# A depthwise convolution's VectorE taps read from a copy in PSUM, with tap counts, weight lows and norm operands moved

## The chip, the cores and the metric

The kernel runs on one core of a Trainium2 chip. The metric is device microseconds (us) of one execution, as a median of several. Engine names are those of the profile: PE is TensorE's matmul row, PEld its weight load, DVE is VectorE, ACT is ScalarE, POOL is GpSimd, SP is SyncE, which issues the loads.

## What is computed

Two blocks follow each other on 256 tokens of 1024 channels, all in float32. The first has two attentions and a retrieval feed-forward; the second has two layers: a differential attention with a Fourier branch and a SwiGLU, and then the convolution module of this study and another SwiGLU. The module, from the reference:

```python
def conformer_conv(h, pw1_w, pw1_b, dw_w, dw_b, ln_g, ln_b, pw2_w, pw2_b):
    a, g = jnp.split(h @ pw1_w + pw1_b, 2, axis=-1)
    u = a * jax.nn.sigmoid(g)
    u = depthwise_conv(u, dw_w) + dw_b
    u = jax.nn.silu(layernorm(u, ln_g, ln_b))
    return u @ pw2_w + pw2_b
```

`depthwise_conv` has 31 taps along the tokens, one set of weights per channel, and zero padding of 15 on both sides.

## The kernel before

Channels lie on the 128 partitions and the 256 tokens along the free dimension, so a 1024-channel tensor is eight tiles of 128x256. Every product of float32 matrices is made of three float32r matmuls: high by high, low by high, high by low, where "high" is the rounded copy of an operand (ACT, `copy`) and "low" the rest (a subtraction, `lo`, L632 and following). Weights stream through four slots: `next_w` loads them (SP), makes the high `wh<-a` on ACT and the low `a<-a,wh` on DVE, and for weights with a cut the last columns of the low on POOL. `self.los` says how many lows are made ahead of the weight that TensorE is using.

`conformer` (L1728) is the part around the change. Its loop goes over j = 0 to 8. In step j, TensorE makes the value product pa(j), then its taps of tile j-1 (`conv_pe`), then the gate product pg(j). ACT takes the sigmoid of pg(j), and DVE makes the input tile u(j) = pa(j) x sigmoid in an SBUF buffer `us` of 286 columns with the padding. The 31 taps of a tile are shared out:

- TensorE (`conv_pe`): the first `PE_TAPS[j]` taps, as float32 matmuls with diagonal matrices that layer 0's feed-forward prepared on ACT.
- ACT and POOL (`conv_pool`): the last `POOL_TAPS[j]` taps. ACT multiplies each into a slot of `taps`; POOL adds the slots in a tree, for 11 taps in four instructions of 1280, 768, 256 and 256 columns.
- DVE (`conv`): the taps between, one instruction each, alternating between two accumulators, `acc` (the output tile y) and `b` (`gb`). The first is a TENSOR_SCALAR, the second adds TensorE's bank, the rest are SCALAR_TENSOR_TENSOR. `finish` then adds `b` and POOL's sum with two TENSOR_TENSORs.

```python
                x = u[:, k:k + T]
                if i == 0 or i == 1 and j == KD - 1:
                    nc.vector.tensor_scalar(acc if i else b, x, dw(j, k), None, op0=ALU.mult)
                elif i % 2 == 1:
                    nc.vector.scalar_tensor_tensor(acc, x, dw(j, k), pc[j][:, :T] if i == 1 else acc, op0=ALU.mult, op1=ALU.add)
```

The order on DVE within step j is: the lows of the two weights of step j+1, u(j), `finish(j-2)`, `conv(j-1)`. On ACT: the sigmoid, the taps of tile j-1, two bias updates of xT, the highs of the next two weights. Each engine runs its list in this order; there is no scheduler.

The layer norm over channels follows: POOL subtracts a rough mean c ahead (`center`), ACT squares, and TensorE adds y and its squares over the partitions with a matrix of ones (`total`) into two banks, `sums`. From these come the mean d and the scale r; y - d, times r, and a Silu on ACT give the tiles for the second projection pw2, whose eight weights follow.

Of the kernel before, what the change touches and what calls it, by code (L numbers as in the profile page):

```python
# [15 lines left out]
AF = mybir.ActivationFunctionType  # L16
ALU = mybir.AluOpType
# [4 lines left out]
D = 1024  # L22
T = 256
# [11 lines left out]
NF = DFF // P  # L35
TAPS = 31
U = KD * T
PE_TAPS = (7, 7, 7, 7, 7, 8, 12, 14)
DIAG = [sum(PE_TAPS[:j]) for j in range(KD)]
POOL_TAPS = (11, 11, 11, 11, 11, 10, 6, 5)  # L40
EARLY = 40
MIDSTEP = 10
MIDS = (1, 2)
# [180 lines left out]
class Done(dict):  # L224
# [5 lines left out]
    def add(self, name):  # L230
        self[name] = max(self.pe.us, self.pe.last) + HOP
# [214 lines left out]
class Net:  # L446
# [85 lines left out]
    def plan(self):  # L532
        a, w = self.a, []
        add = lambda name, cut, *idx: w.append((a[name][idx] if idx else a[name], cut))
        for i in range(6):
            add("w_in", 512, i)
        for i in range(4):
            add("w_sbv", 512, i)
        for kind, i in MAINS:
            if kind == "k":  # L540
                add("w_ukn", 512)
            elif kind == "v":
                add("w_ukv_v", 512)
# [24 lines left out]
        for i in range(KD):
            add("ev_out", 512, (i + 6) % KD)
        for layer in range(2):  # L570
            for f in range(NF + 1):
                if f < NF:
                    add("w1", D, layer, f)
                    add("w3", D, layer, f)
                if f > 0:
                    add("w2", D, layer, f - 1)
            if layer == 0:
                for j in range(KD):
                    add("pw1", PWCUT, j)
                    add("pw1", PWCUT, KD + j)  # L580
                for i in range(KD):
                    add("pw2", 512, i)
        self.w = w
        self.los = 1
        self.w_used = self.w_lo = self.w_hi = self.w_load = self.w_done = 0
        self.raw, self.highs, self.lows = {}, {}, {}
# [1141 lines left out]
    def conformer(self, ctx):  # L1728
# [7 lines left out]
        W = T + TAPS - 1  # L1736
        stat = self.bank("at")
        us = [ar(27648 + i * 288, 288)[:, :W] for i in range(3)]
        taps = [ar(i * 3072, 12, T) for i in range(2)]
        for u in us:  # L1740
            nc.gpsimd.memset(u[:, :half], 0.0)
            nc.gpsimd.memset(u[:, half + T:], 0.0)
# [20 lines left out]
        def conv(j):
            u, acc = us[j % 3], y[:, j]
            second[j] = b = self.t(sp, [P, T], tag="gb", bufs=2)
            for i, k in enumerate(range(PE_TAPS[j], TAPS - POOL_TAPS[j])):
                x = u[:, k:k + T]
                if i == 0 or i == 1 and j == KD - 1:
                    nc.vector.tensor_scalar(acc if i else b, x, dw(j, k), None, op0=ALU.mult)
                elif i % 2 == 1:  # L1770
                    nc.vector.scalar_tensor_tensor(acc, x, dw(j, k), pc[j][:, :T] if i == 1 else acc, op0=ALU.mult, op1=ALU.add)
                else:
                    nc.vector.scalar_tensor_tensor(b, x, dw(j, k), b, op0=ALU.mult, op1=ALU.add)

        def finish(j):
            acc = y[:, j]
            nc.vector.tensor_tensor(acc, acc, second[j], op=ALU.add)
            nc.vector.tensor_tensor(acc, acc, pt[j], op=ALU.add)
            if j == KD - 1:
                nc.vector.tensor_tensor(acc, acc, pc[j][:, :T], op=ALU.add)  # L1780

        sums = [self.bank("at")[:, :T] for _ in range(2)]
        sq = ar(16384, KD, T)
        c, d, d2, r = (ar(25600 + i * T, T) for i in range(4))
        nc.gpsimd.tensor_tensor(gb, self.mods[:, 1, 16:24, 0], self.vec("pw2_b", 0, KD), op=ALU.mult)

        def mean(j):
# [7 lines left out]

        def total(b, e):
            for k in range(b, e):
                for out, x in zip(sums, (y, sq)):  # L1800
                    self.pe.matmul(out, self.con("ones"), x[:, k], start=(k == 0), stop=(k == KD - 1))

        def bias(k):
            nc.scalar.activation(self.xT[:, k], self.xT[:, k], AF.Identity, bias=gb[:, k:k + 1])

        for j in range(KD + 1):
            if j < KD:
                pa = pre.tile()
            if j > 1:
# [47 lines left out]
        square(5, 7)  # L1857
        total(4, 7)
        finish(KD - 1)
        square(KD - 1, KD)  # L1860
        total(KD - 1, KD)
        nc.scalar.activation(d2, sums[0], AF.Square, scale=1.0 / D)
        nc.vector.scalar_tensor_tensor(r, sums[1], 1.0 / D, d2, op0=ALU.mult, op1=ALU.subtract)
        self.copy(d, sums[0], scale=1.0 / D)
        self.act(r, r, AF.Ln, bias=self.eps)
        self.act(r, r, AF.Exp, scale=-0.5)
        self.table(AF.Silu)
        for k in range(KD):
            (nc.vector if k in (0, 1, 3) else nc.gpsimd).tensor_tensor(y[:, k], y[:, k], d, op=ALU.subtract)
        acc = [self.bank("at") for _ in range(4)]  # L1870
        for k in range(KD + 1):
            if k < KD:
                nc.vector.tensor_tensor(y[:, k], y[:, k], r, op=ALU.mult)
                self.act(y[:, k], y[:, k], AF.Silu, scale=self.vec("ln_g", k), bias=self.vec("ln_b", k))
            if k > 0:
                nc.vector.tensor_copy(hh[:, k - 1], y[:, k - 1])
                self.lo(hl[:, k - 1], y[:, k - 1], hh[:, k - 1])
# [202 lines left out]
```

## Time and profile before

| | us |
|---|---|
| runs of before: median (lowest to highest) | 1749.0 (1748.55 to 1751.6) |
| profiled execution, its own time | 1750.69 |
| its span in the profile | 1748.9 |
| busy in the span: PE, DVE, ACT, POOL | 1656.3, 1383.1, 1004.6, 426.9 |
| granted TensorE clock, mean over the span (1 is full) | 0.983 |

The profile's page gives busy time per engine, a span in slices, and the chain of waits that ended last. The whole kernel is mostly TensorE work, so a stage in which TensorE is not busy is what to look for; the stage of the convolution lies from about 1385 to 1544 us in the span. There the useful views are the stretches (busy time per engine in each window), the instructions in order of time on one engine, and the groups of instructions by line. Durations of neighbouring instructions overlap a little, so the distance from start to start is what a queue pays.

### The profile page before, as it was taken

What the parts mean: (1) busy time and instruction counts of PE and PEld (TensorE: products, weight loads), DVE (VectorE), ACT (ScalarE), POOL (GpSimd) and SP (SyncE); (2) the same over time, 40 slices, a digit from 0 to 9 for tenths busy, and PEclk for the clock granted to TensorE, in tenths of its full rate; (3) what the DMA queues carried; (4) which work ended last, traced back from release to release, by engine and by line L of the source; (5) the groups of instructions that cost most, each with busy time, mean ns of one, the idle gap of its engine ahead of it and who ended that gap; (6) DMA issues with size and microseconds to landing.
All of it is one profiled execution on the core that took longest, in us unless ns stands there. A gap on an engine that the chain in (4) does not pass through costs nothing.

```text
span 1748.9 us, 33716 instructions
## 1 busy us (share of the span) xinstructions
PE 1656.3 (95%) x12958; PEld 1582.1 (90%) x12958; DVE 1383.1 (79%) x2399; ACT 1004.6 (57%) x1910; POOL 426.9 (24%) x285
## 2 busy tenths in 40 slices
PE   7989999989999999999999989999999988699998
PEld 6767999989999999999999977789999977599998
DVE  7797899987788866778887688879777799875545
ACT  5755554468777755545554544566555665464444
POOL 3553679900000000000110056432000065420000
PEclk9999999999999999999999999999999998899999
DMA  6332455545445457767878644235888522145553
GB/s 183 117 109 93 138 169 175 187 134 166 161 159 168 157 181 243 239 239 238 311 270 303 231 167 135 70 129 188 309 310 304 193 87 73 37 157 189 185 184 130
DMA packets 88112, 315.66 MB, mean 180 GB/s; under 512 B 10000, under 2 KB 11024, under 8 KB 87696
## 3 DMA queue, kind: packets, MB, share of 16 engines
q1 hardware_dynamic: 87952, 313.51, 53.2%
q8 instruction: 103, 1.69, 0.4%
q14 instruction: 57, 0.47, 0.1%
HBM read 312.03 MB, written 1.05 MB: 179 GB/s over the span
## 4 chain that ended last, share of the span: by engine, by line
PE 64%; DVE 24%; ACT 4%; issue 4%; DMA 2%; POOL 1%; SPq 0%; DVEq 0%; POOLq 0%; ACTq 0%
PE mm L178 34%; PE at L178 30%; DVE a L208 19%; ACT a L208 2%; DMA a<-in_peer_v_dram 1%; ACT wh L208 1%; POOL a L208 1%; DVE gb L208 1%; DVE praw L208 1%; DMA a<-in_w_dram 1%; DVE xT L208 0%; ACT L208 0%; PE at L183 0%; DVE adaw L208 0%; DMA a<-in_w_in_dram 0%
## 5 line engine op out<-in xcount | busy, mean ns | idle before, releaser
L178 PE MATMUL mm<-a,wh 128*128 128x256 f32 (+3 forms) x4752 | 662.0, 289 | 15.6 <-ACT wh L208 9.7
L208 ACT ACTIVATE wh<-a 128x1024 fp32r<-128x1024 f32 (+3 forms) x491 | 515.1, 1053 | 278.4 <-DMA a<-in_w_dram 121.8
L178 PEld LDWEIGHTS mm<-a,wh 128*128 128x128 f32 (+1 forms) x4752 | 607.3, 191 | 31.8 <-ACT wh L208 10.5
L208 DVE TENSOR_TENSOR a<-a,wh 128x1024 fp32r<-128x1024 f32 (+3 forms) x440 | 511.3, 1169 | 113.8 <-ACT wh L208 111.4
L178 PE MATMUL mm<-a,a 128*128 128x256 f32 (+5 forms) x2590 | 420.6, 300 | 39.0 <-DVE a L208 30.2
L178 PEld LDWEIGHTS mm<-a,a 128*128 128x128 f32 (+1 forms) x2590 | 357.9, 193 | 56.0 <-DVE a L208 33.2
L208 POOL TENSOR_TENSOR a<-a,wh 128x512 fp32r<-128x512 f32 (+3 forms) x126 | 239.5, 1912 | 261.1 <-DVE a L208 185.9
L178 PE MATMUL at<-a,wh 128*128 128x256 f32 x2152 | 283.7, 283 | 9.7 <-DVE a L208 5.1
L178 PEld LDWEIGHTS at<-a,wh 128*128 128x128 f32 x2152 | 268.7, 190 | 12.4 <-DVE a L208 6.2
L208 POOL TENSOR_TENSOR a<-a 128x256 f32<-128x256 f32 (+3 forms) x44 | 68.5, 1558 | 742.4 <-ACT a L208 740.5
L178 PE MATMUL at<-a,a 128*128 128x256 f32 (+6 forms) x1288 | 211.6, 299 | 7.0 <-POOL a L208 4.8
L178 PEld LDWEIGHTS at<-a,a 128*128 128x128 f32 (+2 forms) x1288 | 171.6, 191 | 24.2 <-issue 9.1
L208 POOL TENSOR_TENSOR a<-a,a 128x256 f32<-128x256 f32 (+3 forms) x77 | 92.2, 1203 | 310.1 <-ACT a L208 276.2
L208 ACT ACTIVATE a<-a 128x256 fp32r<-128x256 f32 (+6 forms) x223 | 101.2, 464 | 112.2 <-DVE a L208 85.0
L208 DVE TENSOR_TENSOR a<-a,a 128x256 fp32r<-128x256 f32 (+5 forms) x202 | 138.5, 690 | 25.0 <-ACT a L208 21.4
L208 ACT ACTIVATE a<-mm 128x256 f32<-128x256 f32 (+30 forms) x170 | 58.9, 350 | 102.6 <-PE mm L178 102.0
L178 PE MATMUL at<-fgh,wh 128*128 128x256 f32 x352 | 86.3, 282 | 2.2 <-ACT wh L208 2.2
L178 PE MATMUL at<-fgl,wh 128*128 128x256 f32 x352 | 86.1, 282 | 0.0
L208 ACT ACTIVATE oh<-oh,rest 128x128 f16<-128x128 f16 x256 | 80.9, 395 | 0.0
L208 DVE TENSOR_TENSOR a<-a,at 128x176 f32<-128x176 f32 (+48 forms) x111 | 36.2, 352 | 54.4 <-PE at L178 34.7
L208 DVE TENSOR_TENSOR fs<-fs,mm 128x256 f32<-128x256 f32 x38 | 16.0, 421 | 78.2 <-PE mm L178 73.2
L178 PEld LDWEIGHTS at<-fgh,wh 128*128 128x128 f32 x352 | 66.4, 189 | 2.7 <-ACT wh L208 2.7
(153 smaller groups left out, 1603.3 us busy)
## 6 DMA issues: line engine op xcount, KB each, us to landing
a<-in_w_dram SPq DMA_DIRECT2D x132, 512.0 KB, 3.5
a<-in_peer_u_dram SPq DMA_DIRECT2D x128, 512.0 KB, 3.3
a<-in_peer_v_dram SPq DMA_DIRECT2D x128, 512.0 KB, 4.3
adaw<-in_ada_dram SPq DMA_DIRECT2D x48, 512.0 KB, 4.5
a<-in_ada_dram SPq DMA_DIRECT2D x48, 512.0 KB, 4.9
a<-in_pw_dram SPq DMA_DIRECT2D x24, 512.0 KB, 3.2
a<-in_w_pq_dram SPq DMA_DIRECT2D x16, 512.0 KB, 3.3
a<-in_ev_qkf_dram SPq DMA_DIRECT2D x14, 512.0 KB, 3.3
```

What stands on the lines that cost most here:

```text
L178: return self.engine.matmul(out, w, x, **kw)
L208: return f(*args, **kw)
```

## The change

Four things change. The tap counts go from (7, 7, 7, 7, 7, 8, 12, 14) to (7, 8, 8, 8, 8, 8, 11, 14) on TensorE and from (11, 11, 11, 11, 11, 10, 6, 5) to (11, 11, 11, 11, 11, 11, 7, 6) on ACT and POOL. ACT copies u(j) into a PSUM bank, from which DVE's taps read, except the tap that adds TensorE's bank. The lows of pw2 are made wholly on DVE, and the first two of them later. The norm's mean (a second copy, dp) and scale r lie in one PSUM bank, the two sums in another, and POOL subtracts the mean from three tiles where it was five.

```diff
-PE_TAPS = (7, 7, 7, 7, 7, 8, 12, 14)
+PE_TAPS = (7, 8, 8, 8, 8, 8, 11, 14)
-POOL_TAPS = (11, 11, 11, 11, 11, 10, 6, 5)
+POOL_TAPS = (11, 11, 11, 11, 11, 11, 7, 6)
...
-                    add("pw2", 512, i)
+                    add("pw2", D, i)
...
-            u, acc = us[j % 3], y[:, j]
+            acc = y[:, j]
...
-                x = u[:, k:k + T]
+                x = (us[j % 3] if i == 1 and j < KD - 1 else ub[j % 2])[:, k:k + T]
...
-        sums = [self.bank("at")[:, :T] for _ in range(2)]
+        both = self.bank("at")
+        sums = both[:, :T], both[:, T:]
+        ub = [self.bank("at")[:, :W] for _ in range(2)]
...
         for j in range(KD + 1):
+            if j == KD - 1:
+                self.los = 0
...
+            if j < KD:
+                self.copy(ub[j % 2], us[j % 3])
...
         finish(KD - 1)
+        self.los = 2
+        while self.w_lo < self.w_used + 2:
+            self._lo()
...
+        rd = self.bank()
+        r, dp = rd[:, :T], rd[:, T:]
+        self.copy(dp, sums[0], scale=1.0 / D)
+        self.copy(d, sums[0], scale=1.0 / D)
         nc.vector.scalar_tensor_tensor(r, sums[1], 1.0 / D, d2, op0=ALU.mult, op1=ALU.subtract)
-        self.copy(d, sums[0], scale=1.0 / D)
...
-        for k in range(KD):
-            (nc.vector if k in (0, 1, 3) else nc.gpsimd).tensor_tensor(y[:, k], y[:, k], d, op=ALU.subtract)
+        for k in range(2):
+            nc.vector.tensor_tensor(y[:, k], y[:, k], dp, op=ALU.subtract)
+        for k in range(2, KD, 2):
+            nc.gpsimd.tensor_tensor(y[:, k], y[:, k], d, op=ALU.subtract)
+
+        def normal(k):
+            if k > 1 and k % 2 == 1:
+                nc.vector.tensor_tensor(y[:, k], y[:, k], dp, op=ALU.subtract)
+            nc.vector.tensor_tensor(y[:, k], y[:, k], r, op=ALU.mult)
```

ACT's order around one step of the loop, before (the sigmoid of step 4, tile 3's taps into `a_16111`, xT's biases, the next highs):

```order
L208 ACTIVATE gsg_16614<-mm_16589,vecs 128x256
L208 ACTIVATE a_16111<-a_16107,vecs 128x256 x11
L208 ACTIVATE xT<-xT,gbias_16105 128x256 x2
L208 ACTIVATE wh_16652<-a_77 128x1024
L208 ACTIVATE wh_16689<-a_81 128x1024
```

And now, the same step (`at_16125` is one of the two PSUM copies, here of u(4)):

```order
L208 ACTIVATE gsg_16625<-mm_16600,vecs 128x256
L208 ACTIVATE a_16117<-a_16113,vecs 128x256 x11
L208 ACTIVATE at_16125<-a_16114 128x286
L208 ACTIVATE xT<-xT,gbias_16111 128x256 x2
L208 ACTIVATE wh_16663<-a_77 128x1024
L208 ACTIVATE wh_16701<-a_81 128x1024
```

One copy of 286 columns has come in between the taps and the biases, and the highs stand behind it.

DVE's order from u(4) into the taps of tile 3, before (`a_16107` is u(3) in SBUF, `mm_16577` TensorE's bank, `a_16104` the output y):

```order
L208 TENSOR_TENSOR a_224<-a_86,wh_16549 128x1024
L208 TENSOR_TENSOR a_229<-a_90,wh_16586 128x1024
L208 SCALAR_TENSOR_TENSOR a_16108<-mm_16552,vecs,gsg_16614 128x256
L208 TENSOR_TENSOR a_16104<-a_16104,gb_16531 128x256
L208 TENSOR_TENSOR a_16104<-a_16104,a_16110 128x256
L208 TENSOR_SCALAR gb_16634<-a_16107,vecs 128x256
L208 SCALAR_TENSOR_TENSOR a_16104<-a_16107,vecs,mm_16577 128x256
L208 SCALAR_TENSOR_TENSOR gb_16634<-a_16107,vecs,gb_16634 128x256
L208 SCALAR_TENSOR_TENSOR a_16104<-a_16107,vecs,a_16104 128x256
```

And now (`a_16113` is u(3) in SBUF, `at_16126` its PSUM copy, `a_16110` the output y):

```order
L208 TENSOR_TENSOR a_224<-a_86,wh_16559 128x1024
L208 TENSOR_TENSOR a_229<-a_90,wh_16597 128x1024
L208 SCALAR_TENSOR_TENSOR a_16114<-mm_16562,vecs,gsg_16625 128x256
L208 TENSOR_TENSOR a_16110<-a_16110,gb_16542 128x256
L208 TENSOR_TENSOR a_16110<-a_16110,a_16116 128x256
L208 TENSOR_SCALAR gb_16646<-at_16126,vecs 128x256
L208 SCALAR_TENSOR_TENSOR a_16110<-a_16113,vecs,mm_16587 128x256
L208 SCALAR_TENSOR_TENSOR gb_16646<-at_16126,vecs,gb_16646 128x256
L208 SCALAR_TENSOR_TENSOR a_16110<-at_16126,vecs,a_16110 128x256
```

The order is the same. The first tap, and every tap that adds to `gb` or to the output, now reads `at_16126` in place of SBUF; only the tap that adds TensorE's bank `mm_16587` still reads u(3) in SBUF. The two lows and the two additions of `finish` read what they read before.

## Rows read from the trace of the kernel before

**Rows 1.** The page's first part: busy time of each engine, whole span

```profile
PE 1656.3 (95%) x12958; PEld 1582.1 (90%) x12958; DVE 1383.1 (79%) x2399; ACT 1004.6 (57%) x1910; POOL 426.9 (24%) x285
```

**Rows 2.** One stretch; columns: window, length, busy (instructions) by engine, clock, DMA

```profile
1440.00:1460.00 20.00, 15.99 (x103) 14.49 (x101) 19.90 (x32) 10.43 (x23) 11.28 (x7) 0.91 0.24 79
```

**Rows 3.** DVE in order of time, u(3) to u(4), u(7); columns: start, us

```profile
1435.78 0.47 DVE L208 SCALAR_TENSOR_TENSOR a<-mm,vecs,gsg 128x256 f32<-128x256 f32 x1
1437.03 3.00 DVE L208 TENSOR_SCALAR gb<-a,vecs 128x256 f32<-128x256 f32 x1
1444.16 0.47 DVE L208 SCALAR_TENSOR_TENSOR gb<-a,vecs,gb 128x256 f32<-128x256 f32 x1
1444.56 0.47 DVE L208 SCALAR_TENSOR_TENSOR a<-a,vecs,a 128x256 f32<-128x256 f32 x1
1446.94 2.35 DVE L208 TENSOR_TENSOR a<-a,wh 128x1024 fp32r<-128x1024 f32 x2
1449.21 0.47 DVE L208 SCALAR_TENSOR_TENSOR a<-mm,vecs,gsg 128x256 f32<-128x256 f32 x1
1488.90 0.47 DVE L208 SCALAR_TENSOR_TENSOR a<-mm,vecs,gsg 128x256 f32<-128x256 f32 x1
```

**Rows 4.** POOL in order of time: one tree's first addition, then all four

```profile
1436.70 3.18 POOL L208 TENSOR_TENSOR a<-a 128x1280 f32<-128x1280 f32 x1 [6.96 <-ACT a L208]
1436.70 6.86 POOL L208 TENSOR_TENSOR a<-a 128x1280 f32<-128x1280 f32 x4 [6.96 <-ACT a L208]
```

**Rows 5.** Groups of DVE instructions, 1400 to 1512 us: busy, mean, idle

```profile
L208 DVE TENSOR_SCALAR gb<-a,vecs 128x256 f32<-128x256 f32 x8 | 10.5, 1308 | 0.0
L208 DVE SCALAR_TENSOR_TENSOR gb<-a,vecs,gb 128x256 f32<-128x256 f32 x47 | 27.8, 591 | 0.0
L208 DVE SCALAR_TENSOR_TENSOR a<-a,vecs,a 128x256 f32<-128x256 f32 x40 | 22.8, 570 | 0.0
L208 DVE TENSOR_SCALAR a<-a,vecs 128x256 f32<-128x256 f32 x1 | 0.3, 344 | 0.0
L208 DVE TENSOR_TENSOR a<-a,gb 128x256 f32<-128x256 f32 x8 | 9.3, 1167 | 0.0
L208 DVE TENSOR_TENSOR a<-a,a 128x256 f32<-128x256 f32 x8 | 12.1, 1517 | 2.1 <-POOL a L208 1.3
L208 DVE TENSOR_TENSOR a<-a,wh 128x1024 fp32r<-128x1024 f32 x12 | 17.1, 1449 | 0.3 <-ACT wh L208 0.3
L208 DVE SCALAR_TENSOR_TENSOR a<-a,vecs,mm 128x256 f32<-128x256 f32 x7 | 3.3, 470 | 0.0
```

**Rows 6.** PE in order of time: taps, a product's passes, a wait

```profile
1410.00 3.26 PE L178 MATMUL mm<-a,a 128*128 128x256 f32 x14 [1.85 <-DVE a L208]
1412.91 2.25 PE L178 MATMUL mm<-a,wh 128*128 128x256 f32 x16
1415.00 1.11 PE L178 MATMUL mm<-a,a 128*128 128x256 f32 x8
1448.21 6.09 PE L178 MATMUL mm<-a,a 128*128 128x256 f32 x22 [3.44 <-DVE a L208]
```

**Rows 7.** Two stretches of 4 us, before and after that wait

```profile
1440.00:1444.00 4.00, 4.00 (x34) 3.95 (x33) 4.00 (x6) 1.46 (x4) 3.41 (x3) 1.00 0.13 33
1448.00:1452.00 4.00, 3.77 (x13) 3.06 (x14) 4.00 (x4) 2.19 (x3) 4.00 (x1) 0.62 0.31 97
```

**Rows 8.** PE in order of time: the norm's last sums

```profile
1508.88 4.64 PE L178 MATMUL at<-a,cons 128*128 128x256 f32 x10 [6.71 <-ACT a L208]
```

**Rows 9.** ACT in order of time: eleven taps; norm's mean; first Silu

```profile
1442.91 4.59 ACT L208 ACTIVATE a<-a,vecs 128x256 f32<-128x256 f32 x11
1512.70 0.66 ACT L208 ACTIVATE a<-at 128x256 f32<-128x256 f32 x2 [2.42 <-PE at L178]
1517.06 0.60 ACT L208 ACTIVATE a<-a,vecs 128x256 f32<-128x256 f32 x1 [0.72 <-DVE a L208]
```

**Rows 10.** DVE in order of time: the low behind the highs of step 1

```profile
1404.55 1.33 DVE L208 TENSOR_TENSOR a<-a,wh 128x1024 fp32r<-128x1024 f32 x1 [0.34 <-ACT wh L208]
```

More of the change, by code (lines that the diff above doesn't have):

```diff
@@ L1738, in conformer @@
         us = [ar(27648 + i * 288, 288)[:, :W] for i in range(3)]
-        taps = [ar(i * 3072, 12, T) for i in range(2)]
+        taps = [ar(i * 11 * T, 11, T) for i in range(2)]
         for u in us:
@@ L1780, in finish @@
                 nc.vector.tensor_tensor(acc, acc, pc[j][:, :T], op=ALU.add)
-        sums = [self.bank("at")[:, :T] for _ in range(2)]
+        both = self.bank("at")
+        sums = both[:, :T], both[:, T:]
+        ub = [self.bank("at")[:, :W] for _ in range(2)]
         sq = ar(16384, KD, T)
-        c, d, d2, r = (ar(25600 + i * T, T) for i in range(4))
+        c, d, d2 = (ar(25600 + i * T, T) for i in range(3))
         nc.gpsimd.tensor_tensor(gb, self.mods[:, 1, 16:24, 0], self.vec("pw2_b", 0, KD), op=ALU.mult)
@@ L1799, in total @@
             for k in range(b, e):
-                for out, x in zip(sums, (y, sq)):
-                    self.pe.matmul(out, self.con("ones"), x[:, k], start=(k == 0), stop=(k == KD - 1))
+                for i, x in enumerate((y, sq)):
+                    self.pe.matmul(sums[i], self.con("ones"), x[:, k], start=(k == 0 and i == 0), stop=(k == KD - 1 and i == 1))
         def bias(k):
@@ L1867, in conformer @@
         self.table(AF.Silu)
-        for k in range(KD):
-            (nc.vector if k in (0, 1, 3) else nc.gpsimd).tensor_tensor(y[:, k], y[:, k], d, op=ALU.subtract)
+        for k in range(2):
[6 more added lines that the diff above has]
+            nc.vector.tensor_tensor(y[:, k], y[:, k], r, op=ALU.mult)
+            self.act(y[:, k], y[:, k], AF.Silu, scale=self.vec("ln_g", k), bias=self.vec("ln_b", k))
         acc = [self.bank("at") for _ in range(4)]
@@ L1872, in conformer @@
             if k < KD:
-                nc.vector.tensor_tensor(y[:, k], y[:, k], r, op=ALU.mult)
-                self.act(y[:, k], y[:, k], AF.Silu, scale=self.vec("ln_g", k), bias=self.vec("ln_b", k))
+                normal(k)
             if k > 0:
```

## The prediction

> **What bounds the kernel now.** Read the page's first line first: TensorE is busy for 95% of the span [rows 1], so time can be won only where it is not. Next come the stretches. In one that holds a step and a half of the convolution, PE is busy 15.99 of 20 us and DVE 19.90 [rows 2]: here DVE is the bound and TensorE waits for it. Then DVE in order of time. Step j ends with u(j); u(3) starts at 1435.78, u(4) at 1449.21 and u(7) at 1488.90, so the last four steps take 53.1 us, 13.3 each [rows 3]. Within such a step the same kind of instruction takes very different times: the first tap (TENSOR_SCALAR) took 3.00 us, while others took 0.47, spaced 0.40 from start to start [rows 3]. POOL in order of time shows why: a tree starts at 1436.70, its first addition lasts 3.18 us and the whole tree 6.86 [rows 4]. The 3.00 us tap ends at 1440.03, just when that addition does (1439.88).
>
> The groups of DVE instructions make a rule of it [rows 5]. The tap that adds TensorE's bank, with one PSUM input, has a mean of 470 ns in all seven, though POOL works through most of the time. Those with both inputs in SBUF have means of 591 and 570, and the first tap 1308, where the last tile's, beside which POOL has little left, took 344. The excess is 8 x (1.308 - 0.344) = 7.7, 27.8 - 47 x 0.47 = 5.7 and 22.8 - 40 x 0.47 = 4.0: 17.4 us of waiting for POOL in the taps, 2.2 per tile. The two additions of `finish` wait in the same way: 9.3 + 12.1 us for sixteen, at 0.42 each 14.7 too much, 1.8 per tile. The lows took 17.1 us for twelve where an undisturbed pair takes 2.27 (1446.94 to 1449.21 [rows 3]): 3.5 too much, 0.6 per step.
>
> These account for the step: lows 2.27, u 0.40, `finish` 0.85, thirteen taps at 0.40 are 8.7, and 2.2 + 1.8 + 0.6 of waits make 13.3, what was measured.
>
> [...]
>
> **The change part by part.** The sum is made against the profiled execution, 1750.69 us; the median of 1749.0 is 1.7 lower.
>
> *Copy of u and DVE's taps.* In step 1 the copy of u(0) stands on ACT ahead of two highs, whose lows DVE waits for [rows 10]. A copy of 286 columns costs about what a tap on ACT does, 4.59 / 11 = 0.42 us [rows 9]: **+0.4**. In the later steps ACT holds 11 taps, copy, biases, highs of two weights and the sigmoid, some 8 us of a step, with room to spare.
>
> A DVE step has one tap less after the change (31 - 8 - 11 = 12): 8.3 us without waits. TensorE's step: eight taps 2.91 x 8/7 = 3.33, two products at 2.09 + 0.95 = 3.04 each and one matmul of the rough mean (0.24, an estimate from a tap's 2.91 / 14 = 0.21) make 9.65 at full clock [rows 6]. If the rule of [rows 5] holds, the taps' 2.2 us of waits go. What is late next is open: the lows and `finish`, which keep two SBUF inputs each, against POOL's tree. The lower end is no wait there, where TensorE's 9.65 holds the step; the upper end is that they take over all 4.6 us, 12.9 a step. I take their waits as they are, 1.8 + 0.6, nearer to the lower end, because it is the same six instructions beside the same tree [rows 4, 5]: 10.7 per step. TensorE then waits 1.0 us a step, not 3.4, and I let it keep its clock.
>
> Three steps at 10.7 and a last one of 9.2, which TensorE sets (from u(6) on: eleven taps 4.57, the gate product 3.04, then the sigmoid and u, 0.4 each, and the hand-overs between them, an estimate from [rows 3, 6]), are 41.3 instead of 53.1: **-11.8**. From u(1) to u(3) one tile's taps of the disturbed kind fall in (tile 1; at tile 0 the trees have hardly begun), with 2.2 of waits and one tap less, 0.4; I leave 0.2 of it to first taps from PSUM, dearer than 0.34: **-2.4**.
>
> [...] The rows: the tap with a PSUM input takes 470 ns, as long as an undisturbed one from SBUF [rows 3, 5]; its PSUM input, though, is the one that is added, not the shifted one. [...]
>
> *Tail.* From u(7) (1488.90) to the end of the last square sum (1508.88 + 4.64 = 1513.52) it is 24.6 us [rows 3, 8]. DVE has 24 taps of tiles 6 and 7 here, one less than before. Of the two tiles' 4.4 us of waits and 0.4 for the tap I take half: `finish`, the centring on POOL and the squares alternate here and will wait for each other; the sums at the end, ten matmuls in 4.64 us [rows 8], at about half clock, remain as they are. **-2.5**, between 0 and -4.8.
>
> *Norm.* The two sums now share a bank, so the square of the mean on ACT can't start before the last square sum; and three ACT instructions at 0.33 (two took 0.66 [rows 9]) precede r where two did. I put that at +0.95, an estimate from those rows: 0.33 for the third and two square-sum matmuls at half clock. Against it stands that the first Silu waits 0.72 us for DVE behind its table [rows 9], and the subtractions and multiplications that read PSUM there no longer meet POOL. **+0.3**, from -0.5 to +1.2.
>
> *Lows of the second projection.* Two whole ones, 2.3 us, move behind the last `finish`, where DVE has nothing until the sums are done (ten matmuls, 4.64 us [rows 8]). Free; without that cover they cost 2.3. The other six grow on DVE from half to whole, 1.2 us each, beside some 3 us of matmuls per weight [rows 6]. Free. POOL loses these halves. Loads on SP keep their order. Three more diagonal matrices for TensorE's taps are made by ACT in the feed-forward of layer 0, hidden by its matmuls.
>
> The sum: 0.4 - 11.8 - 2.4 - 2.5 + 0.3 = -16.0. 1750.7 - 16.0 = 1734.7, and as a median, 1.7 less, **1733**. The forecast's own range goes from 1727 (steps at TensorE's 9.65, -14.9; tail -4.8; norm -0.5: -22 in all) to 1737 (nothing won in the tail, +1.2 at the norm).
>
> **The rivals.**
> [...]
> 2. *The waits move on.* The lows or `finish` meet POOL's first addition whole, 3.18, where I count half of it or less [rows 4]: 1.8 a step, 7.3 more: 1740; with no gain in the tail 1743. For: they keep two SBUF inputs, and a tree starts when ACT's products are there, not by DVE's time. Against: the taps no longer make POOL wait, so its tree ends sooner.
> 3. *A PSUM input in the shifted place is dearer.* [...] Against: the 470 ns [rows 5]. [...]
> 4. *The change doesn't do what the copy suggests*: the taps do not wait for POOL's reads but for something that ends with them. Then only the taps count, 97 on DVE where there were 103, 2.4 us less, with 0.4 for the copy against it: 1747, no change that can be told.
> 5. *Slower.* POOL's tree (6.86) and the lows and `finish` come to exclude each other entirely, one after the other in each step: 8.3 + 6.9 = 15.2 against 13.3, 1.9 x 4 = 7.6 more, 1757. It decides from the point at which the waits of a step pass 5.0 us (13.3 - 8.3); they are 4.6 now. Against: lows and `finish` stand apart, and the tree's pieces (four additions) let DVE in between.
>
> [...]
>
> **How the numbers follow.** A measurement of this kernel tells 0.2% from no change, 3.5 us: 1745.5 to 1752.5. Chances: the forecast 0.62, rival 1 0.13, rival 2 0.12, rival 3 0.05, rival 4 0.04, rival 5 0.04. All but the last two are faster by over 3.5: 0.92; same 0.04; slower 0.04. The range goes from 1726, just under the forecast's lower end, to 1742, which takes in rivals 1 and 3 and most of rival 2; about 0.15 is left out: rivals 4 and 5, the rest of rival 2 and a little below.
>
> **What would show it.** u(3) to u(7) takes about 41 us, not 53; the taps that read the PSUM copy have a mean of 0.47 and the first one a mean below 0.5; the long instructions are now lows (over 1.2) and the additions of `finish`; there is no wait on PE over 1.5 us within the steps, and a granted clock near 1 in all of them. [...] If u(3) to u(7) takes 50 us or more, the reading of [rows 5] was wrong.

## The result, and the profile after

The changed kernel takes 1727.01 us as a median of four runs (1726.66 to 1729.7), the kernel before 1749.57 beside it: 22.6 us or 1.3% less, the ratio 0.9869 with a 95% interval of 0.9856 to 0.9882. The forecast was 1733, its own range 1727 to 1737; the time lies at the lower end.

The profiled execution took 1729.70 us, 21.0 less than that of before. Of its span of 1727.9 us the first part, up to u(0), is 2.2 us longer than before (u(0) starts at 1401.15, was 1398.98), in a part of the program that the change hardly touches; a second profiled execution of the changed kernel had u(0) at 1397.55. From u(0) on the lengths of the stages repeat: 326.8 and 326.9 us in the two. I therefore compare kernels below from u(0) to the end of the span, stage by stage, and give the median of the whole time beside it. "Tail" is u(7) to the end of the last square sum, "norm" from there to the first matmul of the second projection, "rest" from that to the end; every entry is a difference of two starts or ends in the trace, rounded by itself. The stages come from one profiled execution of each kernel.

| kernel | u(0)-u(1) | u(1)-u(3) | u(3)-u(7) | tail | norm | rest | sum | median us |
|---|---|---|---|---|---|---|---|---|
| before | 10.4 | 26.4 | 53.1 | 24.6 | 4.6 | 230.8 | 349.9 | 1749.6 |
| changed | 10.6 | 21.5 | 38.8 | 20.4 | 4.6 | 230.8 | 326.8 | 1727.0 |
| changed, again | 10.6 | 21.6 | 38.8 | 20.3 | 4.6 | 231.0 | 326.9 | 1726.2 |
| e1, taps from SBUF | 11.0 | 26.0 | 51.1 | 23.7 | 4.6 | 230.9 | 347.4 | 1747.0 |
| e2, probes | 11.0 | 23.4 | 41.0 | 20.2 | 4.6 | 230.9 | 331.1 | 1731.8 |
| e3, before without tree | 10.4 | 16.8 | 38.0 | 16.7 | 5.1 | 230.2 | 317.2 | 1717.5 |
| e4, copy alone | 10.5 | 21.9 | 37.9 | 19.7 | 6.0 | 229.8 | 325.9 | 1732.9 |
| e5, old norm and lows | 10.6 | 23.1 | 39.5 | 20.8 | 6.0 | 231.7 | 331.7 | 1730.3 |
| e6, old counts | 10.6 | 21.9 | 38.0 | 17.4 | 4.6 | 230.8 | 323.3 | 1724.8 |
| e6, again | 10.5 | 21.9 | 37.9 | 18.8 | 4.6 | 231.0 | 324.7 | 1724.4 |
| e8, last step reordered | 11.0 | 23.1 | 38.5 | 19.7 | 4.6 | 230.8 | 327.9 | 1730.1 |
| e9, e6 and e8 | 10.6 | 23.5 | 36.5 | 20.0 | 4.6 | 230.9 | 326.1 | 1727.0 |
| e10, new tail | 10.6 | 21.9 | 38.0 | 15.0 | 4.6 | 231.0 | 321.1 | 1722.9 |

The gain of 23.1 us from u(0) on lies where it was forecast, in the steps and the tail, and nothing is given back later.

DVE in order of time in the changed kernel (start, us, instruction): the low of step 1, then u(3) to u(5), then u(7). These lines stand beside [rows 3, 10]:

```profile
1407.04 1.23 DVE L208 TENSOR_TENSOR a<-a,wh 128x1024 fp32r<-128x1024 f32 x1 [0.67 <-ACT wh L208]
1433.28 0.47 DVE L208 SCALAR_TENSOR_TENSOR a<-mm,vecs,gsg 128x256 f32<-128x256 f32 x1
1443.33 0.47 DVE L208 SCALAR_TENSOR_TENSOR a<-mm,vecs,gsg 128x256 f32<-128x256 f32 x1
1443.72 0.55 DVE L208 TENSOR_TENSOR a<-a,gb 128x256 f32<-128x256 f32 x1
1444.38 0.42 DVE L208 TENSOR_TENSOR a<-a,a 128x256 f32<-128x256 f32 x1
1444.72 0.48 DVE L208 TENSOR_SCALAR gb<-at,vecs 128x256 f32<-128x256 f32 x1
1449.42 3.69 DVE L208 TENSOR_TENSOR a<-a,wh 128x1024 fp32r<-128x1024 f32 x2
1453.04 0.47 DVE L208 SCALAR_TENSOR_TENSOR a<-mm,vecs,gsg 128x256 f32<-128x256 f32 x1
1472.12 0.48 DVE L208 SCALAR_TENSOR_TENSOR a<-mm,vecs,gsg 128x256 f32<-128x256 f32 x1 [2.80 <-ACT gsg L208]
```

u(3) to u(4) is 10.05 us where it was 13.43. The first tap takes 0.48, not 3.00; the additions of `finish` 0.55 and 0.42. Long now are the two lows: 3.69 us, where the pair of [rows 3] took 2.35. The low of step 1 stands 0.67 us behind ACT's highs, 0.33 more than in [rows 10]. Ahead of u(7) DVE has nothing to do for 2.80 us.

The groups of DVE instructions from 1400 to 1495 us (count | busy us, mean ns | idle before) stand beside [rows 5]:

```profile
L208 DVE TENSOR_SCALAR gb<-at,vecs 128x256 f32<-128x256 f32 x8 | 3.8, 476 | 0.0
L208 DVE SCALAR_TENSOR_TENSOR gb<-at,vecs,gb 128x256 f32<-128x256 f32 x42 | 19.9, 473 | 0.0
L208 DVE SCALAR_TENSOR_TENSOR a<-at,vecs,a 128x256 f32<-128x256 f32 x39 | 18.4, 473 | 0.0
L208 DVE TENSOR_TENSOR a<-a,gb 128x256 f32<-128x256 f32 x8 | 6.1, 768 | 0.0
L208 DVE TENSOR_TENSOR a<-a,a 128x256 f32<-128x256 f32 x8 | 4.1, 510 | 3.1 <-POOL a L208 2.0 <-DVE a L208 0.5
L208 DVE TENSOR_TENSOR a<-a,wh 128x1024 fp32r<-128x1024 f32 x14 | 23.5, 1708 | 0.8 <-ACT wh L208 0.8
```

The taps that read the copy have a mean of 473 ns, all 81 of them, so the tap's waits are gone. `finish` is left with 6.1 + 4.1 - 16 x 0.42 = 3.5 us too much in place of 14.7. The lows have 23.5 - 14 x 1.14 = 7.5 too much in place of 3.5. Taken together, what exceeds the undisturbed times was 17.4 + 14.7 + 3.5 = 35.6 us and is 11.0. The first tap is at 476 ns, 132 more than the undisturbed one from SBUF.

The windows of u(3)-u(4), u(4)-u(5), u(5)-u(6) and of the tail (length, then busy us and count of PE, PEld, DVE, ACT, POOL, then the granted clock, DMA share, GB/s) stand beside [rows 2, 7]:

```profile
1433.28:1443.33 10.05, 10.05 (x71) 9.48 (x70) 9.59 (x18) 8.32 (x19) 7.99 (x5) 1.00 0.33 107
1443.33:1453.04 9.71, 9.49 (x65) 8.80 (x64) 9.61 (x18) 7.64 (x18) 7.97 (x5) 1.00 0.32 108
1453.04:1463.14 10.10, 9.93 (x70) 9.23 (x68) 10.00 (x19) 8.41 (x20) 8.00 (x5) 1.00 0.32 105
1472.12:1492.50 20.38, 15.65 (x60) 12.14 (x60) 17.27 (x34) 9.72 (x20) 12.59 (x12) 0.92 0.08 27
```

PE is busy for 29.47 of the three steps' 29.86 us, at full clock, and DVE for 29.20: both queues are now nearly full. Which of them ends a step is seen from the waits. The sigmoids for u(4), u(5) and u(6) ended 2.0 to 2.4 us before these started, behind DVE's lows, while TensorE's taps waited for u(4) and u(6):

```profile
1443.86 3.72 PE L178 MATMUL mm<-a,a 128*128 128x256 f32 x16 [0.22 <-DVE a L208]
1463.66 5.02 PE L178 MATMUL mm<-a,a 128*128 128x256 f32 x22 [0.69 <-DVE a L208]
```

So DVE still ends these three steps, with TensorE close behind. The last step, u(6) to u(7), is TensorE's: there DVE waits 2.80 us for the sigmoid. In the tail the clock is 0.92.

### The profile page after: what moved, and what is told of

The parts are those of the page before. It is cut to its first block, busy times and chain, and to the rows that moved or that the text cites. A ratio compares the mean times of both kernels' runs of the same rounds, so it can differ in the third digit from the quotient of the medians.

```text
span 1727.9 us, 33717 instructions
## 1 busy us (share of the span) xinstructions
PE 1652.9 (96%) x12964; PEld 1580.2 (91%) x12964; DVE 1357.9 (79%) x2395; ACT 1010.0 (58%) x1925; POOL 418.4 (24%) x275
## 4 chain that ended last, share of the span: by engine, by line
PE 63%; DVE 23%; ACT 5%; issue 3%; DMA 3%; POOL 2%; SPq 0%; DVEq 0%; ACTq 0%; POOLq 0%
PE mm L178 34%; PE at L178 28%; DVE a L208 19%; ACT a L208 2%; DMA a<-in_peer_v_dram 2%; ACT wh L208 2%; POOL a L208 1%; DVE praw L208 1%; DMA a<-in_w_dram 1%; DVE xT L208 1%; ACT L208 1%; PE at L183 0%; DVE gb L208 0%; DVE adaw L208 0%; DMA a<-in_w_in_dram 0%
## 5 line engine op out<-in xcount | busy, mean ns | idle before, releaser
L178 PEld LDWEIGHTS mm<-a,wh 128*128 128x128 f32 (+1 forms) x4752 | 608.0, 191 | 33.7 <-ACT wh L208 11.8
L208 DVE TENSOR_TENSOR a<-a,wh 128x1024 fp32r<-128x1024 f32 (+3 forms) x440 | 516.9, 1182 | 118.4 <-ACT wh L208 116.7
L178 PE MATMUL mm<-a,a 128*128 128x256 f32 (+5 forms) x2596 | 415.1, 297 | 24.5 <-DVE a L208 17.7
L178 PEld LDWEIGHTS mm<-a,a 128*128 128x128 f32 (+1 forms) x2596 | 355.2, 191 | 38.5 <-DVE a L208 19.2
L208 POOL TENSOR_TENSOR a<-a,wh 128x512 fp32r<-128x512 f32 (+3 forms) x118 | 228.0, 1943 | 244.9 <-PE at L178 116.8
L208 POOL TENSOR_TENSOR a<-a 128x256 f32<-128x256 f32 (+3 forms) x44 | 73.6, 1673 | 751.4 <-ACT a L208 749.6
L178 PEld LDWEIGHTS at<-a,a 128*128 128x128 f32 (+2 forms) x1288 | 171.5, 190 | 22.6 <-issue 9.1
L208 DVE TENSOR_TENSOR a<-a,a 128x256 fp32r<-128x256 f32 (+5 forms) x191 | 123.7, 648 | 26.0 <-ACT a L208 21.4
L178 PEld LDWEIGHTS at<-fgl,wh 128*128 128x128 f32 x352 | 66.3, 188 | 0.0
```

The source lines that it names most:

```text
L178: return self.engine.matmul(out, w, x, **kw)
L208: return f(*args, **kw)
```

## The experiments

**e1: the copy undone.** Is it the copy, or the counts beside it?

```diff
-                x = (us[j % 3] if i == 1 and j < KD - 1 else ub[j % 2])[:, k:k + T]
+                x = us[j % 3][:, k:k + T]
...
-                self.copy(ub[j % 2], us[j % 3])
```

> The changed kernel with VectorE's taps reading u in SBUF again and no PSUM copy; tap counts, lows and norm as changed. Theory (a tap with both inputs in SBUF waits for POOL's reads, and the copy takes that away): the taps' waits come back, the first tap's mean is again over 1 us, a step is 8.3 + 4.6 = 12.9 us, so u(3) to u(7) takes about 51 and the time is about 1745 us (1740 to 1749). Rival (the eighth tap on TensorE and the new counts bring the gain): 1727 to 1732. Rival (TensorE's clock brings it): 1732 to 1740.

1747.03 us (ten runs), as the theory expected, ratio to before 0.998 (0.9968 to 0.9993). From u(0) on it is 347.4 us, 20.7 more than with the copy. DVE's groups (count | busy us, mean ns):

```profile
L208 DVE TENSOR_SCALAR gb<-a,vecs 128x256 f32<-128x256 f32 x8 | 10.6, 1320 | 0.0
L208 DVE SCALAR_TENSOR_TENSOR gb<-a,vecs,gb 128x256 f32<-128x256 f32 x42 | 27.5, 655 | 0.0
L208 DVE SCALAR_TENSOR_TENSOR a<-a,vecs,a 128x256 f32<-128x256 f32 x39 | 23.3, 597 | 0.0
```

The means of [rows 5] are back (1308, 591, 570 there). So 20.7 of the 23.1 us hang on where the taps read. The rest of the change without it is worth 2.5 us, which fits one tap less per tile on a DVE that is the bound, though no run separates its parts. A clock that rises by itself falls as the cause too: the kernel has everything of the change but the copy.

**e3: POOL's tree left out of the kernel before.** Is it POOL that the taps wait for?

```diff
-            while n > 1:
-                h = n // 2
-                nc.gpsimd.tensor_tensor(p[:, :h], p[:, :h], p[:, n - h:n], op=ALU.add)
-                n -= h
```

> The kernel before without POOL's tree: ACT's products are made but only the first slot is added, so the convolution's sum lacks ten of eleven ACT taps per tile. Nothing else changes: all of VectorE's taps read SBUF. Theory: with POOL silent no tap waits; TENSOR_SCALAR means 0.34, taps 0.47, a step is TensorE's (7 taps 2.91, products 6.08, mean 0.24 = 9.2) or DVE's 8.7, so u(3) to u(7) takes 37 to 40 and the time is 1722 to 1728 us. Rival (the long taps have another cause than POOL): steps stay near 13, time 1745 or more.

1717.49 us, below what was expected (1722 to 1728), ratio 0.9816 (0.9795 to 0.9837). The same DVE groups:

```profile
L208 DVE TENSOR_SCALAR gb<-a,vecs 128x256 f32<-128x256 f32 x8 | 2.8, 345 | 0.0
L208 DVE SCALAR_TENSOR_TENSOR gb<-a,vecs,gb 128x256 f32<-128x256 f32 x47 | 22.4, 478 | 0.0
L208 DVE SCALAR_TENSOR_TENSOR a<-a,vecs,a 128x256 f32<-128x256 f32 x40 | 19.0, 476 | 0.0
```

The taps read SBUF as before and take 478 and 476 ns, the first one 345: POOL's tree makes the taps' waits. Without it even the tail is 16.7 us. u(3) to u(7) takes 38.0 us, as with the copy and seven taps on TensorE (37.9 in e4, 38.0 in e6), but that does not make the tree free once the copy is there: from u(1) to u(7) it is 54.8 us without the tree and 59.8 in e6, so some 5 us of it are left.

**e2: what waits, and for how long.** One instruction that nobody needs, in the midst of POOL's tree, of either kind.

```diff
+                if i == 4:
+                    z = self.t(sp, [P, T], tag="probe", bufs=2)
+                    s = us[j % 3][:, k:k + T]
+                    if j % 2:
+                        nc.vector.tensor_scalar(z, s, dw(j, k), None, op0=ALU.mult)
+                    else:
+                        nc.vector.scalar_tensor_tensor(z, s, dw(j, k), s, op0=ALU.mult, op1=ALU.add)
```

> The changed kernel with one more VectorE instruction per tile, in the middle of the taps while POOL's tree runs, whose result nobody reads: in odd tiles a TENSOR_SCALAR of 256 columns from SBUF (one SBUF input), in even tiles a SCALAR_TENSOR_TENSOR with both inputs in SBUF. Theory A (what waits is any VectorE instruction that takes the way it shares with POOL, the float32 TENSOR_SCALAR included): both kinds take 1 to 3 us each, 1.7 on average over eight, and the time is 1735 to 1742 us. Theory B (only two SBUF inputs wait; the first tap of before was late for another reason): the odd tiles' take 0.3 us, the even ones' 1 to 3, time 1731 to 1735. If neither waits, 0.3 and 0.5 us, time 1729 to 1731.

1731.78 us, which by the total is theory B's range, but only four of the eight probes met the tree, and some of the total has another cause (e8). The single instructions decide. Four of DVE's probes in order of time with one first tap from PSUM between them, and the POOL additions beside the first three lines (start, us):

```profile
1435.92 2.76 DVE L208 SCALAR_TENSOR_TENSOR probe<-a,vecs 128x256 f32<-128x256 f32 x1
1445.42 0.48 DVE L208 TENSOR_SCALAR gb<-at,vecs 128x256 f32<-128x256 f32 x1
1446.99 1.45 DVE L208 TENSOR_SCALAR probe<-a,vecs 128x256 f32<-128x256 f32 x1
1477.33 0.47 DVE L208 SCALAR_TENSOR_TENSOR probe<-a,vecs 128x256 f32<-128x256 f32 x1
1482.82 0.34 DVE L208 TENSOR_SCALAR probe<-a,vecs 128x256 f32<-128x256 f32 x1
```

```profile
1435.47 2.93 POOL L208 TENSOR_TENSOR a<-a 128x1280 f32<-128x1280 f32 x1 [6.22 <-ACT a L208]
1445.32 2.96 POOL L208 TENSOR_TENSOR a<-a 128x1280 f32<-128x1280 f32 x1 [3.29 <-ACT a L208]
```

The probe with two SBUF inputs starts at 1435.92 and ends at 1438.68, just behind POOL's addition, which ends at 1438.40. The TENSOR_SCALAR, one SBUF input, starts at 1446.99 and ends at 1448.44, just behind 1448.28. The other two that met an addition took 2.82 and 1.60 us. The last two lines took 0.47, with POOL idle, and 0.34, started 0.12 us before the end of an addition. Both kinds, as theory A expected, wait until POOL's instruction is about to end. The neighbouring taps, which read the copy and one accumulator in SBUF, take 0.47 beside the same additions.

Of the two TENSOR_SCALARs beside the same POOL addition, the probe, which reads SBUF, takes 1.45 us, and the first tap, which reads PSUM, takes 0.48.

**e4: the copy alone.** The kernel before with the copy and the shared bank of the sums that it needs (added lines alone).

```diff
+                x = (us[j % 3] if i == 1 and j < KD - 1 else ub[j % 2])[:, k:k + T]
...
+        both = self.bank("at")
+        sums = both[:, :T], both[:, T:]
+        ub = [self.bank("at")[:, :W] for _ in range(2)]
...
+                self.copy(ub[j % 2], us[j % 3])
```

> The kernel before with only the PSUM copy of u for VectorE's taps, and the two sums in one bank, which makes room for it; tap counts, lows of the second projection and norm operands as before. Theory (the copy carries the gain): 13 taps make DVE's step 8.7 + 1.6 = 10.3 instead of 9.95, time 1728 to 1731 us. Rival (the new counts are needed because VectorE is still the bound): 1735 or more.

The median was 1732.89 (1726.88 to 1734.27), ratio 0.9896 (0.9871 to 0.9921), 1.9 us above the expected range. In its profile u(0) starts only at 1405.2, 6.2 us later than in that of before, though all code ahead is the same as before; why, is open. From u(0) on it is 325.9 us, 24.1 less than before and 0.9 less than the whole change. A thirteenth tap on DVE did not lengthen the steps: u(3) to u(7) took 37.9, against 38.8 in the changed kernel. What came out worse is the norm, by PE's row of the second projection's first matmul:

```profile
1501.29 4.00 PE L178 MATMUL at<-a,wh 128*128 128x256 f32 x16 [6.00 <-DVE a L208]
```

It waited 6.00 us for DVE; before and in the changed kernel the same gap is 4.6. So the shared bank costs 1.4 us, and mean and scale in PSUM, together with the moved lows, earn it back; no run has one of the two without the other.

**e5: old norm operands and old lows**, with copy and new counts: `r` and `d` in SBUF, five subtractions on POOL, `add("pw2", 512, i)`, no `los = 0`.

> The changed kernel with the norm's mean and scale in SBUF again (five subtractions on POOL) and the second projection's lows as before (half on POOL, two ahead); copy and new tap counts stay, the two sums stay in one bank. Theory from the trace of the copy alone (its norm, from the last square sum to the projection's first matmul, took 5.99 us instead of 4.63, and the rest was 1.0 shorter): norm 6.0, rest 229.8, together 0.4 us longer than the changed kernel, 1726 to 1729 us. Rival (norm operands and lows carry some of the gain): 1731 or more, with the difference after u(7).

1730.30 us (1726.43 to 1732.53), ratio 0.9879 (0.9859 to 0.9899), between the two ranges expected. The norm is 6.0 us again, as in e4. The rest came out at 231.7, in e4 at 229.8 with the same code there: what the lows of the second projection are worth can't be read from this, and stays open. u(1) to u(3) is 1.6 us longer than in the changed kernel, for a reason that e8 shows.

**e6: the old tap counts** (`PE_TAPS` and `POOL_TAPS` of before), everything else as changed; run twice, the second time beside the changed kernel.

> The changed kernel with the tap counts of before (seven taps on TensorE, thirteen on VectorE in the middle tiles). Theory (after the copy TensorE sets the step, 9.6 us of matmuls with eight taps and 9.15 with seven): u(3) to u(7) about 38.0 instead of 38.8, tail a little shorter, 1.0 to 1.5 us faster, 1725 to 1727. Rival (VectorE still sets the step, a tap less on it is 0.4): u(3) to u(7) about 40.4, 1728 to 1730.

> The changed kernel with the tap counts of before, once more. [...] If the first result was chance: no difference.

> The changed kernel once more, unaltered, beside the next two on the same chip, to have its time and its stage lengths twice. From its earlier runs: 1726 to 1730 us, u(3) to u(7) 38.8, tail 20.4, norm 4.6.

1724.77 us (ratio 0.9855, 0.9839 to 0.9872), just below what was expected, then 1724.43 (0.9858, 0.9843 to 0.9873) beside 1726.23 (0.9876, 0.9856 to 0.9895) of the changed kernel. The intervals of the whole times overlap; the stages, which repeat in two profiles of each kernel, don't: u(3) to u(7) is 38.0 and 37.9 against 38.8 in both, the tail 17.4 and 18.8 against 20.4 and 20.3. So by the stages the new counts cost 2 to 3.5 us once the copy is there. In the middle steps two things add up. An eighth tap lengthens TensorE's queue to 9.65 us a step at full clock, by the prediction's estimate: e6 takes 28.1 us from u(3) to u(6), the changed kernel 29.9, and three times 9.65 are 28.95. The other 0.9 us are TensorE's waits for DVE. DVE has one tap more per tile in e6, but shorter lows. Two of e6's three pairs,

```profile
1436.30 2.98 DVE L208 TENSOR_TENSOR a<-a,wh 128x1024 fp32r<-128x1024 f32 x2
1455.82 2.35 DVE L208 TENSOR_TENSOR a<-a,wh 128x1024 fp32r<-128x1024 f32 x2
```

and the third of 3.69 make 9.0 us, where the changed kernel has 3.67, 3.69 and 4.06, 11.4 in all. The pair of 2.35 us started just ahead of one of POOL's 256-column additions, and there it is POOL that waits: that addition takes 2.84 us, where those of the tree of [rows 4] take 0.80 and 0.81. Without its last ten sums the tail is 15.0 us in both profiles of e6 and 16.3 and 16.4 in those of the changed kernel, so some 1.4 us of its difference go with the counts and not with the clock of these sums. The two tails of e6 differ by TensorE's clock: PE's last sums in the first and in the second profile,

```profile
1481.02 0.70 PE L178 MATMUL at<-a,cons 128*128 128x256 f32 x2 [1.94 <-POOL a L208]
1482.88 2.43 PE L178 MATMUL at<-a,cons 128*128 128x256 f32 x10 [1.16 <-ACT a L208]
```

```profile
1479.40 0.70 PE L178 MATMUL at<-a,cons 128*128 128x256 f32 x2 [1.94 <-POOL a L208]
1481.26 3.83 PE L178 MATMUL at<-a,cons 128*128 128x256 f32 x10 [1.16 <-ACT a L208]
```

wait alike, 1.94 and 1.16 us, and take 2.43 in one, at a granted clock of 1.00, and 3.83 in the other, at 0.61.

**e8: another order in step 7.** The gate product ahead of TensorE's taps of tile 6, and ACT's products of tile 6 ahead of the sigmoid.

```diff
-            if j > 1:
+            if j > 1 and j != KD - 1:
                 conv_pe(j - 1)
...
+                if j == KD - 1:
+                    conv_pe(j - 1)
+                    conv_pool(j - 1)
                 self.act(s, pg, AF.Sigmoid, ...)
```

> The changed kernel with another order in step 7 alone: TensorE makes the gate product of tile 7 before its eleven taps of tile 6, and ACT multiplies its seven taps of tile 6 ahead of the sigmoid and the squares of tiles 0 to 3. In the changed kernel VectorE waits 2.8 us there for the sigmoid, and POOL's tree of tile 6 starts at 1478 because ACT's products come after squares that wait for POOL. Theory: u(7) 2 to 3 us earlier, POOL's last trees 4 to 7 us earlier, the last square sum 3 to 6 us earlier: 1721 to 1724 us. Rival (the tail is bound by VectorE's 24 taps and additions after u(7), and its second tap then waits for TensorE's taps): 1726 to 1728.

1730.05 us (ratio 0.9871, 0.9847 to 0.9894), above both ranges expected: nothing won in the whole. ACT's rows show why u(7) came hardly sooner:

```profile
1468.14 2.00 ACT L208 ACTIVATE wh<-a 128x1024 fp32r<-128x1024 f32 x2
1470.03 2.99 ACT L208 ACTIVATE a<-a,vecs 128x256 f32<-128x256 f32 x7
1472.92 0.46 ACT L208 ACTIVATE gsg<-mm,vecs 128x256 f32<-128x256 f32 x1
```

The gate product was ready earlier, but ACT's seven products, which I had put ahead of the sigmoid, ended only at 1473.02, behind highs that ran to 1470.14. A second thing came to light, in a stretch that e8 doesn't touch. TensorE's first taps after u(1), ACT's sigmoid of step 2 and DVE's second addition of `finish` in the changed kernel,

```profile
1412.38 5.38 PE L178 MATMUL mm<-a,a 128*128 128x256 f32 x16 [2.08 <-DVE a L208]
1420.69 0.47 ACT L208 ACTIVATE gsg<-mm,vecs 128x256 f32<-128x256 f32 x1 [2.26 <-PE mm L178]
1425.00 0.42 DVE L208 TENSOR_TENSOR a<-a,a 128x256 f32<-128x256 f32 x1
```

and in e8:

```profile
1412.37 3.69 PE L178 MATMUL mm<-a,a 128*128 128x256 f32 x16 [1.68 <-DVE a L208]
1418.99 0.48 ACT L208 ACTIVATE gsg<-mm,vecs 128x256 f32<-128x256 f32 x1 [0.57 <-PE mm L178]
1425.02 2.96 DVE L208 TENSOR_TENSOR a<-a,a 128x256 f32<-128x256 f32 x1
```

The same sixteen matmuls ran at a granted clock of 0.68 in the changed kernel and of 1.00 in e8, 1.7 us shorter. The sigmoid, and with it ACT's products and POOL's tree, came 1.7 us earlier against u(2), the tree met `finish`, and an addition of 0.42 took 2.96 us; u(2) to u(3) is 11.8 instead of 10.2. The wait depends on where the tree lies against the two additions, and a TensorE that runs ahead puts it on them. The other kernels with the copy fall into the same two groups. In e2, e5 and e9 the clock there is 1.00 and the second addition takes 2.94, 2.95 and 2.93; in the changed kernel again, e4, e6 (twice) and e10 it is 0.65 to 0.68 and the addition takes 0.42 or 0.43. Both groups have waits of about 2 us ahead of these taps (1.68 to 2.04 and 1.97 to 2.08), so what decides the clock is not resolved. From u(3) to the end of the tail, the part that the new order touches, e8 takes 58.3 us and the changed kernel 59.2 and 59.1.

**e9: e6 and e8 together.**

> The changed kernel with both the tap counts of before and the new order of step 7. If the two add up: 1.0 to 1.5 us and 3 to 5 us, 1720 to 1723 us. If the twelve taps of tile 6 on TensorE hold VectorE's second tap after the new order: no better than the new order alone, 1722 to 1725.

1727.03 us (ratio 0.9862, 0.9845 to 0.9878), no better than e6 alone and above both ranges expected. From u(3) to u(7) it is 1.4 to 1.5 us shorter than e6 (36.5), but u(1) to u(3) is 1.6 us longer, at full clock as in e8, and the tail 1.2 to 2.6 (20.0). One reason in the tail is PE's last ten sums, which waited 3.34 us and took 4.63, at a clock of 0.50.

**e10: a new tail on the old counts.** Here the idle time is filled instead of shortened: DVE's 2.8 us ahead of u(7) take six taps of tile 6, ACT's wait for the sigmoid takes its products of tile 6, and POOL centres what the last addition needs first. TensorE's order stays.

```diff
+                if j == KD - 1:
+                    conv_pool(j - 1)
+                    conv(j - 1, 0, 6)
                 self.act(s, pg, AF.Sigmoid, ...)
...
-                elif j == 7:
-                    square(0, 3)
-                    square(3, 4)
...
             elif j == 8:
+                square(0, 3)
+                square(3, 4)
                 total(0, 4)
...
-        center(KD - 2, KD - 1)
         nc.gpsimd.tensor_tensor(pt[KD - 1], pt[KD - 1], c, op=ALU.subtract)
+        center(KD - 2, KD - 1)
```

> The same tap counts of before, with another order at the end: VectorE makes six of tile 6's thirteen taps in its 2.7 us of waiting for the last sigmoid, ACT makes its six products of tile 6 ahead of that sigmoid, the squares of tiles 0 to 3 come after ACT's last products, and POOL centres the last tile's sum before tile 6. Theory (what ends last in the tail is the chain ACT products, POOL trees, two additions on VectorE): u(7) unchanged, the last square sum 3 to 4 us earlier, 1720 to 1722 us. Rival (the tail is TensorE's taps of tile 7 and its sums, or the clock falls): less than 1.5 us gained, 1723 to 1726.

1722.86 us (1719.07 to 1725.44), ratio 0.9852 (0.9837 to 0.9867), between the two ranges expected. It is the fastest of the kernels that compute the whole convolution, 3.4 below the changed kernel beside it. The tail is 15.0 us, 2.4 to 3.8 less than e6's and 5.3 less than the changed kernel's. DVE's u(7), the last addition that waited for POOL, and PE's last sums:

```profile
1466.72 0.48 DVE L208 SCALAR_TENSOR_TENSOR a<-mm,vecs,gsg 128x256 f32<-128x256 f32 x1 [0.43 <-ACT gsg L208]
1478.11 0.73 DVE L208 TENSOR_TENSOR a<-a,a 128x256 f32<-128x256 f32 x1
```

```profile
1479.27 2.43 PE L178 MATMUL at<-a,cons 128*128 128x256 f32 x10 [0.95 <-ACT a L208]
```

DVE waits 0.43 us for the sigmoid instead of 2.80, the last addition of POOL's sum takes 0.73 with no idle time ahead of it, and the sums take 2.43, the shortest seen. Without these sums the tail is 12.5 us, where e6 has 15.0 in both profiles. Against e6 alone the medians (1.6 apart) don't separate; the stage lengths do.

## Why the prediction was right, and where its sizes were off

Direction, place and mechanism held: the taps waited out POOL's instructions (e3: the first tap 345 ns without the tree, 1308 with it; e2), the copy took that away (473 ns, and 655 and 597 in e1 without it), and the gain lies between u(1) and the last square sum. The size was 7.1 us short: -23.1 us from u(0) on, where the terms said -16.0, and 1.6 of the 7.1 are luck (u(1) to u(3), below). The forecast's own range, added up from its terms, ends at 1736 rather than 1737.

- **Copy in step 1, +0.4**: measured +0.2 (10.4 to 10.6), but e1, without the copy, has 11.0 there, so the stage varies by more than the copy could cost, and its price isn't shown.
- **The middle steps, -11.8**: measured -14.3. The term that was off is "I take their waits as they are, 1.8 + 0.6", the lows and `finish` beside the same tree. They are 1.65: u(3) to u(6) takes 9.95 a step, 8.3 of it DVE's work without waits. Some 1.4 of it is the lows' and 0.3 that of `finish`. The tree did the same work, but in another place. Before, ACT was 6.3 us ahead of DVE (products of tile 3 from 1442.91 [rows 9], u(4) at 1449.21 [rows 3]), and POOL was at work through all of 1448 to 1452 [rows 7], when `finish` stood there. ACT and POOL in the changed kernel:

```profile
1440.46 0.48 ACT L208 ACTIVATE gsg<-mm,vecs 128x256 f32<-128x256 f32 x1 [1.73 <-PE mm L178]
1440.84 4.59 ACT L208 ACTIVATE a<-a,vecs 128x256 f32<-128x256 f32 x11
1496.17 1.09 ACT L208 ACTIVATE a<-a,vecs 128x256 f32<-128x256 f32 x2
```

```profile
1445.50 8.21 POOL L208 TENSOR_TENSOR a<-a 128x1280 f32<-128x1280 f32 x4 [1.51 <-ACT a L208]
```

  The products start at 1440.84, 2.5 us ahead of u(4), and the tree at 1445.50, just after the two additions of `finish` (1443.72 to 1444.80). What it meets is the next lows at 1449.42. With DVE's step shorter, ACT is no longer far ahead of it, and that puts the tree between `finish` and the lows. POOL waits as well: its two 256-column additions take 1.60 us each beside the lows (from 1450.43 and from 1452.11), where the tree of [rows 4] has them at 0.80 and 0.81, and the tree lasts 8.21 us, not 6.86. The sum's lower end, TensorE's 9.65 a step, came nearest, but TensorE does not end the steps: with the waits for u(4) and u(6) it comes to 9.95 as well.
- **u(1) to u(3), -2.4**: measured -4.9, u(2) to u(3) alone -4.0. I had counted 2.2 us of the taps' waits here and none of `finish`, the same mistake. But 1.6 of the 4.9 are luck. They go with the low clock of TensorE's taps after u(1) (e8); in e5 and e8, whose code is the same there and whose clock stayed at 1.00, the stage takes 23.1, 3.3 less than before. Of the signs that the prediction names, "no wait on PE over 1.5 us" and "a granted clock near 1" fail in this stretch: 2.08 us and 0.68.
- **Tail, -2.5 between 0 and -4.8**: measured -4.2. Of it 0.6 is the last ten sums, 4.05 us instead of 4.64. The other 3.6 show that the loss to POOL, which I expected to take half of 4.8, is smaller. The sums at the end kept a low clock, as I said (0.59, before 0.50). PE's rows:

```profile
1487.11 0.70 PE L178 MATMUL at<-a,cons 128*128 128x256 f32 x2 [3.21 <-POOL a L208]
1488.46 4.05 PE L178 MATMUL at<-a,cons 128*128 128x256 f32 x10 [0.65 <-ACT a L208]
```

  After 3.21 and 0.65 us of waiting, the last ten sums take 4.05 us; [rows 8] had 4.64.
- **Norm, +0.3**: measured 0.0, from two parts that e4 and e5 show apart, +1.4 for the shared bank and -1.4 for operands in PSUM together with the moved lows. The first Silu starts at 1496.17 with no wait behind its table, the slack I had counted on.
- **Lows of the second projection, 0**: the rest of the kernel is 230.8 in both. That moving them was harmless is shown, what it is worth isn't.
- **One tap less on DVE**: I priced it as 0.4 per step on DVE and left out what it does to TensorE's queue and to the place of the tree. The part of the change without the copy, this tap with it, was worth 2.5 us (e1); with the copy the new counts cost 2 to 3.5 (e6).

Of the rivals, the first (TensorE's clock falls in every step, as to 0.62 in [rows 7]) fell: the granted clock is 1.00 in the windows from u(3) to u(6). A fall as before would have cost 1.7 us a step, an estimate from [rows 6]: 6.09 - (3.26 + 1.11), the latter two at a clock of 1.00. The second was half right: the lows' waits doubled (3.5 to 7.5 us), but `finish` paid for them (14.7 to 3.5). The third fell with 473 ns against 470, and against 478 and 476 for the taps from SBUF in e3: an input in PSUM beside one in SBUF made these taps no dearer. No run shows what it would have cost. Only the first tap is dearer, 476 against 344; why, no run shows. The fourth fell with e1, the fifth by its sign.

## What to carry to other kernels

Where VectorE's small instructions that read two operands from SBUF show means far above their shortest (here 591 and 570 ns against 470, the first tap 1308 against 344), lay them beside GpSimd's instructions in order of time; if their ends coincide, give them an input in PSUM, even by a copy on an engine that has room (here the means fell to 473 and 476). After such a wait is gone, draw up the step anew before tuning counts: here both queues were then nearly full (PE 29.47 and DVE 29.20 of 29.86 us), and the new counts, a tap moved to TensorE among them, cost 2 to 3.5 us, where the change without the copy had earned 2.5. Waits between engines depended on phase here, that is on where the one engine's burst lay against the other's instructions: the same addition took 0.42 us in the changed kernel and 2.96 in e8. So price what remains of them from both sides rather than as it was, and before comparing two kernels by a stage, see that the stages ahead of it are in the same phase in both.

## What was not expected of the hardware

- A lower clock made a stage shorter: with TensorE's taps after u(1) at 0.65 to 0.68 of the clock, u(2) to u(3) took 10.2 to 10.6 us; at 1.00, in kernels with the copy, 11.8 to 12.1, because POOL's tree then met `finish`.
- The same ten sum matmuls took between 2.43 and 4.64 us in the kernels here; after equal waits (e6 and its repeat) 2.43 and 3.83. The granted clock there was 1.00 in the one and 0.61 in the other; what sets it, these runs don't resolve.
- A part of the program that runs nearly the same instructions can differ by some microseconds between executions (u(0) from 1396.0 to 1405.2), while stages of the convolution repeated to 0.1 us in the two profiles of the changed kernel. Stage lengths told apart what medians couldn't.
